# Own addresses for the seven feed-forward products

## The chip, the cores and the metric

The kernel runs on one core of one Trainium2 chip. The metric is the time of one execution on the device in microseconds (us); of several runs the median is given. TensorE multiplies matrices into the eight PSUM banks, VectorE (DVE) and ScalarE (ACT) work on tiles, GpSimd (POOL) does so too and issues some DMAs, SyncE (SP) issues most of them. SBUF holds 128 partitions; every address below is the byte address inside a partition.

## The reference

One layer of an encoder runs on two sequences (`x_prompt`, `x_sample`), each 1024 rows of 1024 numbers, with one set of float32 weights. Every sub-layer is shifted, scaled and gated by vectors that come from a conditioning input.

```python
h = rmsnorm(x, g_mix) * (1.0 + sc1) + sh1
z = h @ w_in                                   # latents for attention, and the Fourier input
mix = concatenate([mla_group(...), fourier_group(...)], axis=-1) @ w_out
x = x + ga1 * mix
h2 = rmsnorm(x, g_ffn) * (1.0 + sc2) + sh2
ffn = (silu(h2 @ w_gate) * (h2 @ w_up)) @ w_down   # 1024 -> 2816 -> 1024
return rmsnorm(x + ga2 * ffn, g_final)
```

The feed-forward part, the line with `w_gate`, `w_up` and `w_down`, is what the change touches.

## The kernel before

The kernel works in stages: weight preparation and projections, the Fourier part, attention with the output projection, and the feed-forward part. The feed-forward part runs from about 740 us to the end, first for sequence 0, then for sequence 1.

*Split operands.* Each float32 operand is held as two tiles, a rounded high part and the rest (`split`, lines 62 to 64: a cast on ACT, a subtraction on DVE). One product of two tiles is then three matmuls into the same bank (`mm3`, lines 79 to 81): high by high, high by low, low by high. In a matmul the first operand is the stationary 128x128 one that a weight load brings into the array ahead of it, the second the moving one of 512 columns.

*Seven products.* Each matrix product is done on 2x2 blocks in a form with seven block products and a few additions (numbers 0 to 6). In the first stage the moving operands are seven combinations of the normalised input, H[0] to H[6]. Each is held in two tiles (`H00` high, `H01` low, and so on) of 4 slices with 512 columns. They are made once per sequence by `prep_h` and stay. The stationary operands are combinations of `w_gate` and `w_up` for one block of 128 columns: seven tiles of 128x512, made into high and low parts by `hl` in buffers that turn through eight of each kind, `wh` and `wl`.

*First stage.* A sequence takes 22 passes. A pass does the products in the order 0, 5, 1, 6, 4, 3, 2 (`step`), 4 slices of 3 matmuls each, 12 matmuls a product, and uses three banks: x and y are added to again two products later, z likewise. Behind each product, `step` makes one tile of the next pass's weights with `hl`, and then a result is read out of a bank on ACT (lines 1704 and 1711) or DVE (line 1708 and `add`). Raw weights come by SP into four slots `X0` to `X3` (`slot`), two per pass, and POOL forms their sums. Results go to DRAM (`s_d`) by SP and POOL.

*Second stage.* `prod2` does one product of the down projection in 11 steps. Each step loads a tile a from `s_d` and a tile b from `w_down` or its sums, splits both with `hl` and does 4 x 3 matmuls: a gives the stationary slices, b is the moving tile. Seven products are 77 steps for sequence 0. Sequence 1 has 66, and its last product is done from tiles that were split ahead into H tiles that are no longer needed (`prep_last`, 132 matmuls). At the end of sequence 0, the weights for the first pass of sequence 1 are split by the line with `first_w`.

*Places.* Tiles lie in pools, one behind the other: H tiles and slots X on the left side of SBUF, `wh`, `wl`, two small tiles (`gf`, `tdb`) and 18 turning `val` tiles on the right. All H, X, wh and wl tiles are multiples of 512 bytes long, and all of them start at 64 modulo 512.

*Order.* The engines' programs are in the order that the framework's planner gives them. It places an instruction by when its operands are due. `issue_after` and `first` hold single instructions back.

Of the kernel before, what the change touches and what calls it, by code (L numbers as in the profile page):

```python
# [12 lines left out]
F32 = mybir.dt.float32  # L13
F32R = mybir.dt.float32r
# [7 lines left out]
P = 128  # L22
# [25 lines left out]
NTE = 258  # L48
NT = 514
NX = 2 * (NCOS + NNYQ)  # L50


@with_exitstack
def hybrid_encoder_kernel(ctx: ExitStack, tc: tile.TileContext, a: dict):
# [117 lines left out]
    zo = zp.tile([ZOW, NZC], F32, name="zo")  # L172
    zx = zp.tile([P, NX], F32, name="zx")
    zp.tile([P, 120], F32, name="gapz")
# [5 lines left out]
    with ExitStack() as st:  # L180
        p1b = st.enter_context(ExitStack())
        w2 = p1b.enter_context(tc.tile_pool(name="p1b", bufs=1, side="right", reuse_waits="tile"))
        w = st.enter_context(tc.tile_pool(name="p1", bufs=1, reuse_waits="tile"))
# [648 lines left out]
    S = {}  # L832
# [98 lines left out]
    with ExitStack() as st:  # L931
        early = st.enter_context(ExitStack())
        wa = early.enter_context(tc.tile_pool(name="p2a", bufs=1, reuse_waits="tile"))
        w = st.enter_context(tc.tile_pool(name="p2", bufs=1, side="right", reuse_waits="tile"))
# [293 lines left out]
    with ExitStack() as st:  # L1228
        w = st.enter_context(tc.tile_pool(name="p3", bufs=1, side="right", reuse_waits="tile"))
# [116 lines left out]
        for k in range(nit + 4):  # L1346
            if k >= nit:
                i = k - nit
# [7 lines left out]
            if k < nit:  # L1356
                s, b, h, u = items[k]
                scores(s, b, h, u)
                nxt = items[k + 8 - k % 8] if k + 8 - k % 8 < nit else None
                i = k % 8  # L1360
# [11 lines left out]
            if 0 <= k - 2 < nit and (k - 2) % 4 == 3:  # L1372
                s, b, h, u = items[k - 2]
# [17 lines left out]
    with ExitStack() as st:  # L1391
        w = st.enter_context(tc.tile_pool(name="p5", bufs=1, reuse_waits="tile"))
# [6 lines left out]
        def quad(tag, dt=F32):  # L1399
            return w.tile([P, 4, 512], dt, tag=tag, name=tag, bufs=1)  # L1400

        def slot(i, name="draw"):
            return w.tile([P, 2, 512], F32, tag=f"X{i % 4}", name=name, bufs=1)


        for tag in ("H20", "X0", "X1", "H21", "H30", "H31", "H00", "H41", "H01", "H50", "H51", "H10", "H11", "H40", "H60", "H61"):
            quad(tag) if tag[0] == "H" else [slot(2 * int(tag[1]) + i) for i in range(2)]

        def prep_h(H, s, n):

# [91 lines left out]
        H = {}  # L1502
# [13 lines left out]
        with tc.issue_after(S.pop(("tail", 4))):  # L1516
            w0 = sums_w([r[i // 2][:, i % 2, :] for i in range(4)], lambda i: wc[:, i, :], nc.vector)
# [27 lines left out]
        w5 = st.enter_context(tc.tile_pool(name="p5b", bufs=1, side="right", reuse_waits="tile"))  # L1545
# [5 lines left out]
        def val():  # L1551
            return w5.tile([P, 512], F32, tag="v", name="val", bufs=VALS)

        def hl(v):
            h = w5.tile([P, 512], F32R, tag="wh", name="wh", bufs=8)
            if "gf" not in S:
                S["gf"] = w5.tile([P, D], F32, name="gf")
                w5.tile([P, 2, 512], F32, tag="ga", name="tdb", bufs=1)
            l = w5.tile([P, 512], F32R, tag="wl", name="wl", bufs=8)
            split(h, l, v)  # L1560
            return h, l

        gf, first_w = None, None
        order = [fi + half * (NF // 2) for fi in range(NF // 2) for half in range(2)]
        pending = []
        turn = [0]
        for s in range(2):
            def combos(n, first=False, ahead=0):
                f = order[n]
# [68 lines left out]
                store_s(2, fi, v4, nc.gpsimd)  # L1638

            if s == 0:  # L1640
                wts = [hl(w0[i]) for i in range(4)]
                with behind():
                    for _ in range(2):
                        next(prep)
            else:
                wts = first_w
            A = {}
            late = None
            for n, f in enumerate(order):
                cur, nxt = wts, []  # L1650
                src = combos(n + 1, s == 0 and n == 0) if n + 1 < NF else None
                if late is not None:
                    put_s(*late)
                    late = None
                elif s == 0 and n > 0:
                    down_combos(n // 2)
                    if n % 4 == 1 and n < 20:
                        comb_h(1, n // 4 - 1) if n >= 5 else None

                def step(j, ps, k, first, src=src):  # L1660
                    prod(ps, k, cur[j], first)
                    if s == 0 and n == 0:
                        if j == 0:
                            cur.extend(hl(v) for v in w0[4:])
                            w0.clear()
                            S["n3"] = norm3(1, S.pop("jk3").bitcast(BF16))
                        if j < 3:
                            with behind():
                                for _ in range(2):
                                    next(prep, None)  # L1670
                            if j == 1:
                                with behind():
                                    S.pop("n3")()
                            return
                        if j == 3:
                            src = S["w1"] = sums_w(src, lambda i: val(), nc.vector)
                        src = S["w1"]
                        for i in ((), (), (), (0, 1), (2, 3), (4,), (5, 6))[j]:
                            nxt.append(hl(src[i]))
                        if j == 6:  # L1680
                            flip2(3, [S.pop(("xn", 1, 3, u)) for u in range(2)], bank, lambda g: val())
                    elif s == 1 and n == 0:
                        if j == 2:
                            with tc.issue_after(here["u2"]):
                                S["w1"] = sums_w(src, lambda i: val(), nc.vector)
                        with behind(), tc.issue_after(here["c"]) if j > 1 else ExitStack():
                            for i in ((), (), (0,), (1, 2), (3,), (4,), (5, 6))[j]:
                                nxt.append(hl(S["w1"][i]))
                        if j == 6:
                            S.pop("w1")  # L1690
                    elif src is not None:
                        nxt.append(hl(src[j]))
                    if s == 0 and n == 1 and j == 2:
                        S.pop("w1", None)

                def pend():
                    if pending:
                        with behind():
                            pending.pop(0)()

                x, y, z = bank(), bank(), bank()
                step(0, x, 0, True)
                p1 = val()
                here["c"] = nc.scalar.copy(p1, x).ins
                pend()
                step(1, y, 5, True)
                u2 = val()
                here["u2"] = nc.vector.tensor_tensor(out=u2, in0=y, in1=p1, op=ALU.add).ins  # L1708
                step(2, x, 1, False)
                sg = val()  # L1710
                nc.scalar.activation(sg, x, AF.Silu)
                pend()
                step(3, y, 6, False)
                u3 = val()
                add(u3, y, p1, nc.vector)
                step(4, z, 4, True)
                add(u3, z, u3, nc.vector)
                pend()
                step(5, y, 3, False)
                add(p1, y, p1, nc.vector)  # L1720
                nc.scalar.activation(p1, p1, AF.Silu)
                nc.vector.tensor_tensor(out=u3, in0=p1, in1=u3, op=ALU.mult)  # L1722
                step(6, z, 2, False)
                add(u2, z, u2, nc.vector)
                nc.vector.tensor_tensor(out=u2, in0=sg, in1=u2, op=ALU.mult)
                A[0, n % 2] = u2
                A[1, n % 2] = u3
                if n % 2 == 1:
                    late = (n // 2, A)
                    A = {}  # L1730
                wts = nxt
            put_s(*late)
            ga = w5.tile([P, D], F32, tag="ga", name="ga2", bufs=1)
            if gf is None:
                gf = S["gf"]
# [49 lines left out]
            def prod2(ps, k, first, last, hook=None, skip=0):  # L1785
                for f in range(NF // 2):
                    if f == NF // 2 - 1:
                        turn[0] -= skip
                    raw = slot(turn[0])
                    turn[0] += 1 + (skip if f == NF // 2 - 1 else 0)  # L1790
                    nc.sync.dma_start(raw[:, 0, :], s_d[s][k, f])
                    nc.sync.dma_start(raw[:, 1, :], bsrc(k, f))
                    ah, al = hl(raw[:, 0, :])
                    bh, bl = hl(raw[:, 1, :])
                    for t in range(4):
                        tt = slice(t * P, t * P + P)
                        mm3(ps[t], ah[:, tt], al[:, tt], bh, bl, first and f == 0, last and f == NF // 2 - 1, not first)
                    if hook is not None:
                        hook(f)
# [126 lines left out]
                    S["w0"] = combos(0, ahead=1)  # L1926

            prod2(Z, 2, False, True, hooks(steps, first_combos), 2)
            first_w = [hl(v) for v in S.pop("w0")]
            pending = rows_out(c11, u2, 0, 1, Z)  # L1930
            X = Y = Z = None
            H = Hn
# [109 lines left out]
```

## Time and profile before

| | |
|---|---|
| three runs | 2016.7, 2016.65, 2015.29 us; median 2016.65 us |
| profiled execution | span 2015.8 us from the first to the last instruction; the profile gives no other time for it |
| TensorE busy | 1973.1 us (98%), weight loads 1620.0 us (80%) |
| DVE, ACT, POOL busy | 1390.5 us (69%), 889.0 us (44%), 849.8 us (42%) |
| granted TensorE clock, mean | 0.995 |
| DMA | 376.59 MB, 187 GB/s on average |

A row of a group reads: line, engine, operation, written tile <- read tiles, shape, count, then the total and the mean time of one instruction, then the idle time of the engine ahead of them and what ended it. A row of a timeline reads: start and duration in us, engine, line, operation, tiles. Matmuls overlap on TensorE, so that the time of one is longer than the step from one start to the next; that step is called the pitch below. A row of windows reads: from:to, length, TensorE's busy time and its count of matmuls (any that reach into the window), granted clock, share and rate of the DMA engines.

### The profile page before, as it was taken

What the parts mean: (1) busy time and instruction counts of PE and PEld (TensorE: products, weight loads), DVE (VectorE), ACT (ScalarE), POOL (GpSimd) and SP (SyncE); (2) the same over time, 40 slices, a digit from 0 to 9 for tenths busy, and PEclk for the clock granted to TensorE, in tenths of its full rate; (3) what the DMA queues carried; (4) which work ended last, traced back from release to release, by engine and by line L of the source; (5) the groups of instructions that cost most, each with busy time, mean ns of one, the idle gap of its engine ahead of it and who ended that gap; (6) DMA issues with size and microseconds to landing.
All of it is one profiled execution on the core that took longest, in us unless ns stands there. A gap on an engine that the chain in (4) does not pass through costs nothing.

```text
span 2015.8 us, 27568 instructions
## 1 busy us (share of the span) xinstructions
PE 1973.1 (98%) x9526; PEld 1620.0 (80%) x9526; DVE 1390.5 (69%) x2064; ACT 889.0 (44%) x1720; POOL 849.8 (42%) x1012
## 2 busy tenths in 40 slices
PE   6899999999999999999999999999999999999998
PEld 3778778888888877888888888888888888888886
DVE  4557757766687678777777567788755655656784
ACT  2665535555565563333333356453333333335541
POOL 0654312111223237779779410344644554420152
PEclk8999999999999999999999999999999999999999
DMA  9785884445553575645646597665333333267762
GB/s 385 262 318 193 283 331 114 122 94 121 150 123 105 188 256 197 205 158 198 202 155 202 176 314 230 230 229 185 126 99 100 107 103 105 99 203 242 251 228 86
DMA packets 179449, 376.59 MB, mean 187 GB/s; under 512 B 17996, under 2 KB 57548, under 8 KB 175468
## 3 DMA queue, kind: packets, MB, share of 16 engines
q1 hardware_dynamic: 156908, 305.60, 45.3%
q0 software_dynamic: 21824, 68.17, 11.3%
q8 instruction: 75, 1.23, 0.2%
q10 hardware_dynamic: 576, 1.05, 0.1%
q14 instruction: 66, 0.54, 0.1%
HBM read 262.75 MB, written 120.39 MB: 190 GB/s over the span
## 4 chain that ended last, share of the span: by engine, by line
PE 59%; DVE 2%; issue 1%; POOL 1%; ACT 0%; POOLq 0%; DVEq 0%; ACTq 0%
PE bank L80 20%; PE bank L79 20%; PE bank L81 20%; DVE wl L64 1%; DVE val L152 0%; DVE val L1834 0%; DVE H L64 0%; DVE val L1806 0%; POOL rs_y L107 0%; DVE val L149 0%; POOL out_dram L1840 0%; DVE val L1722 0%; POOL rs_w L109 0%; POOL rs_w L110 0%; DVE val L1708 0%
## 5 line engine op out<-in xcount | busy, mean ns | idle before, releaser
L79 PE MATMUL bank<-H,wh 128*128 128x512 f32 x1232 | 480.8, 390 | 3.0 <-DVE val L152 1.3
L80 PE MATMUL bank<-H,wh 128*128 128x512 f32 x1232 | 480.0, 390 | 0.3 <-DVE H L64 0.3
L81 PE MATMUL bank<-H,wl 128*128 128x512 f32 x1232 | 479.8, 390 | 0.2 <-DVE wl L64 0.2
L79 PEld LDWEIGHTS bank<-H,wh 128*128 128x128 f32 x1232 | 231.4, 188 | 53.7 <-DVE val L152 2.6
L64 DVE TENSOR_TENSOR wl<-draw,wh 128x512 fp32r<-128x512 f32 x286 | 208.1, 764 | 90.9 <-ACT wh L63 90.2
L80 PEld LDWEIGHTS bank<-H,wh 128*128 128x128 f32 x1232 | 231.4, 188 | 48.4 <-DVE H L64 0.6
L81 PEld LDWEIGHTS bank<-H,wl 128*128 128x128 f32 x1232 | 231.4, 188 | 48.3 <-DVE wl L64 0.5
L152 DVE TENSOR_TENSOR val<-bank,val 128x512 f32<-128x512 f32 x200 | 136.6, 689 | 162.9 <-PE bank L81 162.3
L63 ACT CAST wh<-draw 128x512 fp32r<-128x512 f32 x286 | 165.1, 619 | 174.2 <-PE bank L80 129.4
L152 POOL TENSOR_TENSOR val<-val 128x512 f32<-128x512 f32 x58 | 81.0, 1398 | 344.2 <-DVE val L1806 164.5
L80 PE MATMUL bank<-wl,wh 128*128 128x512 f32 x572 | 223.3, 390 | 0.9 <-DVE wl L64 0.9
L81 PE MATMUL bank<-wh,wl 128*128 128x512 f32 x572 | 222.8, 390 | 0.0
L79 PE MATMUL bank<-wh 128*128 128x512 f32 x572 | 222.8, 389 | 0.0
L63 ACT CAST wh<-rgu 128x512 fp32r<-128x512 f32 x172 | 107.0, 622 | 257.4 <-PE bank L80 202.7
L63 ACT CAST wh<-val 128x512 fp32r<-128x512 f32 x133 | 82.2, 621 | 262.1 <-PE bank L80 244.9
L64 DVE TENSOR_TENSOR wl<-val,wh 128x512 fp32r<-128x512 f32 x133 | 125.7, 947 | 66.7 <-ACT wh L63 66.7
L64 DVE TENSOR_TENSOR wl<-rgu,wh 128x512 fp32r<-128x512 f32 x172 | 165.4, 961 | 1.4 <-ACT wh L63 1.4
L149 POOL TENSOR_TENSOR val<-rgu 128x512 f32<-128x512 f32 x80 | 107.8, 1347 | 79.4 <-DMA rgu<-in_wgu_dram 75.7
L80 PEld LDWEIGHTS bank<-wl,wh 128*128 128x128 f32 x572 | 107.5, 188 | 24.7 <-DVE wl L64 2.6
L79 PEld LDWEIGHTS bank<-wh 128*128 128x128 f32 x572 | 107.4, 188 | 22.5
L81 PEld LDWEIGHTS bank<-wh,wl 128*128 128x128 f32 x572 | 107.4, 188 | 21.9
L149 POOL TENSOR_TENSOR val<-val 128x512 f32<-128x512 f32 x89 | 119.3, 1358 | 1.3
(400 smaller groups left out, 3897.8 us busy)
## 6 DMA issues: line engine op xcount, KB each, us to landing
rgu<-in_wgu_dram SPq DMA_DIRECT2D x86, 512.0 KB, 4.0
draw<-s_d SPq DMA_DIRECT2D x143, 256.0 KB, 3.3
s_d<-val POOLq DMA_DIRECT2D x88, 256.0 KB, 3.2
draw<-t_d SPq DMA_DIRECT2D x88, 256.0 KB, 4.4
s_d<-val SPq DMA_DIRECT2D x66, 256.0 KB, 3.7
draw<-in_w_down_dram SPq DMA_DIRECT2D x55, 256.0 KB, 4.0
wada<-in_w_ada_dram SPq DMA_DIRECT2D x11, 1024.0 KB, 9.3
xt<-in_x_dram SPq DMA_DIRECT2D x16, 512.0 KB, 10.8
```

Of the source, the lines that this page charges most:

```text
L63: here["a"] = nc.scalar.copy(hi, src).ins
L64: here["v"] = (eng or nc.vector).tensor_tensor(out=lo, in0=src, in1=rd(hi), op=ALU.subtract).ins
L79: nc.tensor.matmul(out, lh, rh, start=first, stop=False, skip_group_check=cont)
L80: nc.tensor.matmul(out, lh, rl, start=False, stop=False, skip_group_check=cont)
L81: here["t"] = nc.tensor.matmul(out, ll, rh, start=False, stop=last, skip_group_check=cont).ins
L149: return eng.tensor_tensor(out=out, in0=x, in1=y, op=ALU.subtract).ins
L152: eng.tensor_tensor(out=out, in0=x, in1=y, op=ALU.add)
```

## The change

H tiles get untouched gaps in front of them, so that both tiles of H[k] start at `PLACE[k]` modulo 512. Each weight tile of the first stage gets a slot of its own, `wh0` to `wh6` and `wl0` to `wl6`, in the order of the products of a pass, at the place of its product; an eighth slot of each kind lies at 64. `hl` takes the number of the slot. In the second stage the tiles a and b take slots 0 and 1, then 2 and 3, 4 and 5, 6 and 7, and so on around (`spin`). `gf` and `tdb` stay between the two kinds, and are now placed when the pool is opened. No instruction, load or store is added or left out.

```diff
+PLACE = (64, 0, 32, 96, 128, 256, 160)
...
+        at = 64
+
+        def shift(pool, to):
+            nonlocal at
+            gap, at = (to - at) % 512, to
+            if gap:
+                pool.tile([P, gap // 4], F32, name=f"gap{len(gaps)}")
+                gaps.append(gap)
+
+        gaps = []
         for tag in ("H20", "X0", "X1", "H21", "H30", "H31", "H00", "H41", "H01", "H50", "H51", "H10", "H11", "H40", "H60", "H61"):
-            quad(tag) if tag[0] == "H" else [slot(2 * int(tag[1]) + i) for i in range(2)]
+            if tag[0] == "H":
+                shift(w, PLACE[int(tag[1])])
+                quad(tag)
+            else:
+                for i in range(2):
+                    slot(2 * int(tag[1]) + i)
...
-        def hl(v):
-            h = w5.tile([P, 512], F32R, tag="wh", name="wh", bufs=8)
-            if "gf" not in S:
+        spots = [PLACE[k] for k in (0, 5, 1, 6, 4, 3, 2)] + [64]
+        at = 64
+        for kind in "hl":
+            for i, spot in enumerate(spots):
+                shift(w5, spot)
+                w5.tile([P, 512], F32R, tag=f"w{kind}{i}", name=f"w{kind}", bufs=1)
+            shift(w5, 64)
+            if kind == "h":
                 S["gf"] = w5.tile([P, D], F32, name="gf")
                 w5.tile([P, 2, 512], F32, tag="ga", name="tdb", bufs=1)
-            l = w5.tile([P, 512], F32R, tag="wl", name="wl", bufs=8)
+
+        def hl(v, i):
+            h = w5.tile([P, 512], F32R, tag=f"wh{i}", name="wh", bufs=1)
+            l = w5.tile([P, 512], F32R, tag=f"wl{i}", name="wl", bufs=1)
             split(h, l, v)
             return h, l
...
-                        nxt.append(hl(src[j]))
+                        nxt.append(hl(src[j], j))
...
-                    ah, al = hl(raw[:, 0, :])
-                    bh, bl = hl(raw[:, 1, :])
+                    ah, al = hl(raw[:, 0, :], spin[0])
+                    bh, bl = hl(raw[:, 1, :], spin[0] + 1)
+                    spin[0] = (spin[0] + 2) % 8
...
-            first_w = [hl(v) for v in S.pop("w0")]
+            first_w = [hl(v, i) for i, v in enumerate(S.pop("w0"))]
```

More of the change, by code (lines that the diff above doesn't have):

```diff
@@ L1566, in hybrid_encoder_kernel @@
         turn = [0]
+        spin = [0]
         for s in range(2):
@@ L1640, in hybrid_encoder_kernel @@
             if s == 0:
-                wts = [hl(w0[i]) for i in range(4)]
+                wts = [hl(w0[i], i) for i in range(4)]
                 with behind():
@@ L1663, in step @@
                         if j == 0:
-                            cur.extend(hl(v) for v in w0[4:])
+                            cur.extend(hl(v, 4 + i) for i, v in enumerate(w0[4:]))
                             w0.clear()
@@ L1678, in step @@
                         for i in ((), (), (), (0, 1), (2, 3), (4,), (5, 6))[j]:
-                            nxt.append(hl(src[i]))
+                            nxt.append(hl(src[i], i))
                         if j == 6:
@@ L1687, in step @@
                             for i in ((), (), (0,), (1, 2), (3,), (4,), (5, 6))[j]:
-                                nxt.append(hl(S["w1"][i]))
+                                nxt.append(hl(S["w1"][i], i))
                         if j == 6:
```

## The prediction

> **What bounds the kernel now.** I read the page first: the shares of the span, the granted clock, the chain that ended last and the costliest groups.
>
> ```profile
> span 2015.8 us, 27568 instructions
> PE 1973.1 (98%) x9526; PEld 1620.0 (80%) x9526; DVE 1390.5 (69%) x2064; ACT 889.0 (44%) x1720; POOL 849.8 (42%) x1012
> PEclk8999999999999999999999999999999999999999
> PE bank L80 20%; PE bank L79 20%; PE bank L81 20%; DVE wl L64 1%; DVE val L152 0%; DVE val L1834 0%; DVE H L64 0%; DVE val L1806 0%; POOL rs_y L107 0%; DVE val L149 0%; POOL out_dram L1840 0%; DVE val L1722 0%; POOL rs_w L109 0%; POOL rs_w L110 0%; DVE val L1708 0%
> L79 PE MATMUL bank<-H,wh 128*128 128x512 f32 x1232 | 480.8, 390 | 3.0 <-DVE val L152 1.3
> L80 PE MATMUL bank<-wl,wh 128*128 128x512 f32 x572 | 223.3, 390 | 0.9 <-DVE wl L64 0.9
> L79 PE MATMUL bank<-H 128*128 128x512 f32 x44 | 17.1, 389 | 0.0
> ```
>
> TensorE is busy for 98% of the span at full clock, and 60% of the last chain is the lines 79 to 81 on `bank`, the feed-forward. Each of the three lines issues 1232 matmuls in the first stage (inputs H against weights wh, wl), 572 in the second, 44 at the end: 3 x 1848 = 5544. Their own 390 ns overlap, so what counts is the pitch from start to start. I took it from windows without a stall (a count holds some two matmuls that only reach into the window).
>
> ```profile
> 1450.00:1790.00 340.00, 340.00 (x1501) 1.00 0.32 106
> 1805.00:1950.00 145.00, 145.00 (x641) 1.00 0.76 252
> ```
>
> 340 us over 1499 is 226.8 ns in the first stage, 145 over 639 is 226.9 in the second: one pitch, whatever the DMA share (0.32 and 0.76). At it, 5544 matmuls are 1257 us. A nanosecond of pitch is 5.5 us, 0.27% of the span. Everything here hangs on whether the pitch knows addresses.
>
> Two views say that it is not a constant. The first is the timeline behind a stall.
>
> ```profile
> 926.78 0.40 PE L80 MATMUL bank<-H,wh 128*128 128x512 f32 x1
> ...
> 929.10 0.39 PE L81 MATMUL bank<-H,wl 128*128 128x512 f32 x1
> ```
>
> Ten pitches lie between these two rows: 2.32 us, 232.0 ns each, the same form as above. After a stall the pitch is thus 5 ns worse for some ten matmuls and then falls back to 226.8: a good rhythm that has to be found again, at about 10 x 5.2 = 52 ns for this one.
>
> The second is the Fourier input projection, where 128x256 slices of `wcs` run against `eoh` and `eol`. A row of `wcs` chunks is 536 floats, so each chunk of three matmuls starts 96 bytes further modulo 512. These are chunks one and six, twice, some 21 us apart.
>
> ```profile
> 94.40 0.28 PE L79 MATMUL bank<-wcs_h,eoh 128*128 128x256 f32 x1
> 94.78 0.28 PE L79 MATMUL bank<-wcs_h,eoh 128*128 128x256 f32 x1
> 96.19 0.28 PE L79 MATMUL bank<-wcs_h,eoh 128*128 128x256 f32 x1
> 96.53 0.28 PE L79 MATMUL bank<-wcs_h,eoh 128*128 128x256 f32 x1
> 115.44 0.28 PE L79 MATMUL bank<-wcs_h,eoh 128*128 128x256 f32 x1
> 115.81 0.28 PE L79 MATMUL bank<-wcs_h,eoh 128*128 128x256 f32 x1
> 117.22 0.28 PE L79 MATMUL bank<-wcs_h,eoh 128*128 128x256 f32 x1
> 117.56 0.28 PE L79 MATMUL bank<-wcs_h,eoh 128*128 128x256 f32 x1
> ```
>
> Three matmuls take 0.38 and 0.37 us at the first chunk, 0.34 and 0.34 at the sixth: 127 and 123 ns against 113 each. The difference comes back with the address, so a moving stream and the weight load beside it do depend on where they lie.
>
> **The change, part by part.** (a) *Inside a product of the first stage.* Before, H and weights all start at 64 modulo 512 (the diff's bookkeeping starts there). After, H[k] and the slots of product k share PLACE[k], so the distance between moving and stationary tile stays 0, and slices move by 2048 and 512 bytes, which keep it. If only the distance matters, 3696 matmuls stay at 226.8. No row shows a shared place other than 64, so the bounds: upwards the 5.2 ns above; downwards the 128x448 projection, one form in two states.
>
> ```profile
> 98.47 0.37 PE L79 MATMUL bank<-wz_h,eoh 128*128 128x448 f32 x1
> 100.75 0.37 PE L81 MATMUL bank<-wz_h,eol 128*128 128x448 f32 x1
> 106.00 0.36 PE L79 MATMUL bank<-wz_h,eoh 128*128 128x448 f32 x1
> 107.42 0.37 PE L80 MATMUL bank<-wz_l,eoh 128*128 128x448 f32 x1
> ```
>
> Eleven pitches in 2.28 us are 207.3 ns, seven in 1.42 us are 202.9: 4.4 ns lower. Six of seven products move, 3168 matmuls: -13.9 to +16.5 us. I take 0. The `wz` slices alternate between two places 256 bytes apart and hold 207.3, which speaks for a pitch that a shift alone does not alter.
>
> (b) *Switches of product.* 2 x 22 x 7 = 308 times the moving start jumps, and during the last matmul of one product the weights of the next load from another place. A rhythm that is lost costs up to the 52 ns above: 0 to 16.0 us, below nothing only with (a). I take one switch in six at 52 ns: +2.7 us, nearer to 0 because one odd load is less than a stall.
>
> (c) *The second stage.* The pair of slots for a and b goes round 64/256, 0/160, 128/96, 32/64, so the distance is no longer 0 in any pair: 1716 matmuls. By the same bounds -7.6 to +8.9 us. I take half of the upper one, +4.5 us: the one 128x512 rhythm that the trace shows away from 226.8 is the 232.0 ns one, and the address does matter by the `wcs` rows, but some pairs may find the better rhythm. The last product keeps both its operands in one H tile, 132 matmuls: 0, with 0.6 us on either side by the same bounds.
>
> (d) *Seven slots for eight turning buffers.* The cast of next weights j had the buffer of product j-1, and now waits for product j itself.
>
> ```profile
> 1000.05 0.39 PE L79 MATMUL bank<-H,wh 128*128 128x512 f32 x1
> 1000.08 0.62 ACT L63 CAST wh<-rgu 128x512 fp32r<-128x512 f32 x1 [1.59 <-PE bank L80]
> 1000.83 0.68 DVE L1708 TENSOR_TENSOR val<-bank,val 128x512 f32<-128x512 f32 x1
> 1001.43 1.18 DVE L64 TENSOR_TENSOR wl<-rgu,wh 128x512 fp32r<-128x512 f32 x1
> 1002.77 0.39 PE L79 MATMUL bank<-H,wh 128*128 128x512 f32 x1
> ```
>
> A product is 2.72 us. ACT already waits for TensorE at every product and casts 0.03 us into the next one; VectorE empties the bank before it subtracts. One product later the same beat carries the next tile, used five products on instead of six: 5 x 2.72 = 13.6 us against some 2.6 us (1000.08 to 1002.61). 0. Behind it on SP stand the loads of `rgu`, which wait for that subtraction, and then POOL's sums: all move by 2.72 us with their consumer, so no slack is used. If VectorE's order turned, it would cost (rival four).
>
> (e) *The seam between the sequences.* The first casts of sequence two ran ahead of the last tile of sequence one.
>
> ```profile
> 1375.98 0.62 ACT L63 CAST wh<-val 128x512 fp32r<-128x512 f32 x1
> 1376.11 0.69 DVE L64 TENSOR_TENSOR wl<-val,wh 128x512 fp32r<-128x512 f32 x1
> 1376.33 0.39 PE L81 MATMUL bank<-wh,wl 128*128 128x512 f32 x1
> 1376.56 0.39 PE L79 MATMUL bank<-H,wh 128*128 128x512 f32 x1
> 1376.58 0.62 ACT L63 CAST wh<-rgu 128x512 fp32r<-128x512 f32 x1
> 1376.71 0.69 DVE L64 TENSOR_TENSOR wl<-rgu,wh 128x512 fp32r<-128x512 f32 x1
> ```
>
> With 77 tiles the pair index ends at 76 x 2 modulo 8 = 0, so the last tile sits in slots 0 and 1, and the cast into slot 0 waits for its last read: start at 1376.58 instead of well before, end 1377.20, subtraction to about 1378.0. The third matmul needs it and would have started at 1376.56 + 2 x 0.227 = 1377.01: +1.0 us (0.6 to 1.2). Behind it on ACT the other casts follow at half a microsecond, faster than a product uses them.
>
> (f) *Gaps.* No instruction, no DMA. The tiles lie up to 2 KB further on the left, up to 4 KB lower on the right, over other old tiles; the stage's entry can shift by the idle time of L79 above, 3.0 us, at most: I take 0, -1 to +1.
>
> Sum: 0 + 2.7 + 4.5 + 0 + 1.0 + 0 = +8.2 us on a span of 2015.8, 2024.0. The median of the runs, 2016.65, stands 0.85 above that span (which is all that the profile gives of its execution's time): 2024.9, rounded down to 2024 because most of the sum rests on lost rhythm, whose terms can share a cause.
>
> **Rivals.** *No change in pitch.* Only (e) is left: 2016.65 + 1.0 = 2017.7. For it: one pitch in both stages under all loads. Against: the `wcs` rows. The Trainium skill, page "TensorE: Matmul & The Clock Gate", section "Step-by-step: what each phase is for", says that TensorE reads moving data and weights through two independent ports, so that the next weight load takes nothing from the running matmul; by that rule this rival is the outcome, and the `wcs` rows (127 against 113 ns by place) do not agree with it.
>
> *Faster.* One mechanism: a place other than 64 gives a pitch as much lower as the 128x448 states differ, in half of the moved products: 1584 x 4.4 ns = 7.0 us, less the 1.0 of (e): 2010.7; in all, and in the second stage too, 2016.65 - 13.9 - 7.6 + 1.0 = 1996. It decides from 1.3 ns a matmul on those 3168. Against: 226.8 is the lowest pitch that any 128x512 row here shows.
>
> *Much slower.* Every switch and every pair loses the rhythm, and shifted places too: 2016.65 + 16.5 + 16.0 + 8.9 + 1.0 = 2059; switches and pairs alone, 2042.6.
>
> *VectorE between bank and bank.* If it subtracted first, the bank would be empty at 0.03 + 0.62 + 1.18 + 0.68 = 2.51 us of a product's 2.72, and a slow subtraction would stop TensorE: 0.3 us in 44 passes, 13 us, 2030. Against: the order in the rows of (d).
>
> **How the numbers follow.** Forecast 0.45; no change in pitch 0.31; faster 0.18; much slower 0.04; VectorE 0.02. About 0.2%, 4 us, is what a measurement of this kernel can tell from no change: below 2012.6 lies most of "faster", 0.17; within, the second case and the edge of the first and third, 0.33; above, 0.50. The forecast's own range is 2020 to 2033 (2.7 and 4.5 replaced by their upper halves: 8.0 + 6.7 + 1.0 = 15.7). The range for 8 in 10 takes in the second case and the milder half of the third: 2008 to 2033.
>
> **What would show it.** A window inside the first stage at 226.8 for every product shows (a) right; a product with its own pitch, wrong. Pitches near 232 in the first matmuls after each switch show (b). Windows of the second stage: 145 us over some 632 matmuls show (c) in part, over 639 show it wrong. At the seam a stall of 1 us before the third matmul shows (e). The waits of ACT for L80 should keep their total, and L1708 should stand before L64. What would make the prediction wrong is a pitch that follows the place itself and not the distance.

## The result, and the profile after

The changed kernel takes 2033.3 us (median of 4 runs, 2030.95 to 2036.84) against 2016.68 for the kernel before beside it (2015.29 to 2016.8, 4 runs): a ratio of 1.0083, 95% interval 1.0071 to 1.0095. That is 16.6 us more, where 2024, some 8 us more, was forecast. The profiled execution took 2033.57 us with a span of 2031.5, 15.7 us above the span of before.

The page after has the same picture as before. Its lines are numbered one higher (`mm3` is now 80 to 82).

```profile
span 2031.5 us, 27501 instructions
PE 1990.9 (98%) x9526; PEld 1619.4 (80%) x9526; DVE 1399.6 (69%) x2064; ACT 889.8 (44%) x1720; POOL 845.1 (42%) x1012
L80 PE MATMUL bank<-H,wh 128*128 128x512 f32 x1232 | 481.6, 391 | 1.8 <-DVE val L1733 0.7
L81 PE MATMUL bank<-wl,wh 128*128 128x512 f32 x572 | 226.4, 396 | 0.4 <-DVE wl L65 0.2
```

TensorE carries 17.8 us more busy time with the same 9526 matmuls, more than the whole added span. No engine took over, and the waits did not grow in sum: idle time ahead of the six groups of matmuls of the two stages is 4.2 us, against 4.4 before (1.8 and 0.4 us ahead of the two shown). A matmul's own time went from 390 to 391 ns in the first stage and from 390 to 396 in the second. The windows give the pitch. The columns are from:to, length, TensorE's busy time with its count, granted clock, DMA share and rate.

```profile
1450.00:1790.00 340.00, 340.00 (x1488) 1.00 0.31 103
1815.00:1950.00 135.00, 135.00 (x581) 1.00 0.74 243
```

Less the two matmuls that only reach in, 340 us over 1486 is 228.8 ns in the first stage (226.8 before) and 135 over 579 is 233.2 in the second (226.9). The granted clock is 1.00 in both, so TensorE's clock was not lower: each matmul starts later after the one ahead of it.

The timeline shows where. These are the first matmuls of the seven products of one first-stage pass, and of the next pass (start and duration in us).

```profile
1538.43 0.39 PE L80 MATMUL bank<-H,wh 128*128 128x512 f32 x1
...
1541.17 0.39 PE L80 MATMUL bank<-H,wh 128*128 128x512 f32 x1
...
1543.90 0.39 PE L80 MATMUL bank<-H,wh 128*128 128x512 f32 x1
...
1546.63 0.39 PE L80 MATMUL bank<-H,wh 128*128 128x512 f32 x1
...
1549.40 0.39 PE L80 MATMUL bank<-H,wh 128*128 128x512 f32 x1
...
1552.16 0.39 PE L80 MATMUL bank<-H,wh 128*128 128x512 f32 x1
...
1554.90 0.39 PE L80 MATMUL bank<-H,wh 128*128 128x512 f32 x1
...
1557.64 0.39 PE L80 MATMUL bank<-H,wh 128*128 128x512 f32 x1
```

The pass takes 19.21 us, against 84 x 226.7 = 19.04. In six of the seven products the pitch starts out longer and comes back to 227 ns after three to nine matmuls; product 1 has it from its first. The excess is in the matmuls around the switches, in four cases in the last one ahead of a switch too (235 to 237 ns). Taken from the trace's starts as medians over 19 passes of sequence two, the switches cost 34, 12, 0, 51, 32, 32 and 12 ns (into products 0, 5, 1, 6, 4, 3, 2): 0.174 us a pass.

In the second stage the pitch never settles at 227. These are the first matmuls of five tiles in turn; the pairs lie at 0/160, 128/96, 32/64 and 64/256 (weights/moving).

```profile
1874.56 0.39 PE L80 MATMUL bank<-wh 128*128 128x512 f32 x1
...
1877.37 0.39 PE L80 MATMUL bank<-wh 128*128 128x512 f32 x1
...
1880.15 0.40 PE L80 MATMUL bank<-wh 128*128 128x512 f32 x1
...
1882.95 0.39 PE L80 MATMUL bank<-wh 128*128 128x512 f32 x1
...
1885.75 0.39 PE L80 MATMUL bank<-wh 128*128 128x512 f32 x1
```

Four tiles take 11.19 us: 48 matmuls at 233.1 ns. The seam between the sequences has the new stall.

```profile
1382.57 0.40 PE L82 MATMUL bank<-wh,wl 128*128 128x512 f32 x1
1382.82 0.62 ACT L64 CAST wh<-rgu 128x512 fp32r<-128x512 f32 x1 [0.28 <-PE bank L81]
...
1383.49 0.51 PE L80 MATMUL bank<-H,wh 128*128 128x512 f32 x1 [0.53 <-ACT wh L64]
...
1383.83 0.39 PE L81 MATMUL bank<-H,wh 128*128 128x512 f32 x1
1384.06 0.46 PE L80 MATMUL bank<-H,wh 128*128 128x512 f32 x1
...
1384.36 0.50 PE L82 MATMUL bank<-H,wl 128*128 128x512 f32 x1
```

The cast into a slot of the last tile is released by that tile's L81 and ends at 1383.44; TensorE waits for it. Over the four long steps that follow 1382.57, TensorE loses 0.99 us.

The difference of the two traces, by the starts of the 5544 feed-forward matmuls (us):

| stretch | before | after | difference |
|---|---|---|---|
| up to the first feed-forward matmul | 740.01 | 738.49 | -1.5 |
| sequence one, first stage | 425.96 | 427.85 | +1.9 |
| sequence one, second stage | 210.59 | 217.14 | +6.6 |
| sequence two, first stage | 420.05 | 423.92 | +3.9 |
| sequence two, second stage | 180.41 | 185.14 | +4.7 |
| last product, from the H tiles | 29.69 | 30.16 | +0.5 |
| behind the last matmul | 9.09 | 8.75 | -0.3 |

The pitch accounts for 7.3 + 11.0 + 0.5 = 18.8 us (mean of the steps under 260 ns, less that of before, times 3696, 1716 and 132). Longer steps, the stalls, are 1.2 us less in sum, the seam included, and the rest is the two ends. Since the first feed-forward matmul of the kernels below falls anywhere from 736.5 to 740.3 us, those 1.5 us are not put down to the change.

### The profile page after: what moved, and what is told of

The parts are those of the page before. It is cut to its first block, busy times and chain, and to the rows that moved or that the text cites. A ratio compares the mean times of both kernels' runs of the same rounds, so it can differ in the third digit from the quotient of the medians.

```text
span 2031.5 us, 27501 instructions
## 1 busy us (share of the span) xinstructions
PE 1990.9 (98%) x9526; PEld 1619.4 (80%) x9526; DVE 1399.6 (69%) x2064; ACT 889.8 (44%) x1720; POOL 845.1 (42%) x1012
## 4 chain that ended last, share of the span: by engine, by line
PE 60%; DVE 2%; POOL 1%; DMA 0%; issue 0%; ACT 0%; SPq 0%; POOLq 0%; DVEq 0%; ACTq 0%
PE bank L81 20%; PE bank L82 20%; PE bank L80 20%; DMA draw<-in_w_down_dram 0%; DVE wl L65 0%; DVE val L1832 0%; DVE val L1750 0%; DVE val L153 0%; DVE H L65 0%; POOL rs_y L108 0%; DVE val L150 0%; POOL out_dram L1866 0%; ACT wh L64 0%; POOL rs_w L110 0%; POOL rs_w L111 0%
## 5 line engine op out<-in xcount | busy, mean ns | idle before, releaser
L81 PE MATMUL bank<-H,wh 128*128 128x512 f32 x1232 | 481.9, 391 | 1.3 <-DVE H L65 1.3
L81 PEld LDWEIGHTS bank<-H,wh 128*128 128x128 f32 x1232 | 231.4, 188 | 52.3 <-DVE H L65 1.5
L81 PE MATMUL bank<-wl,wh 128*128 128x512 f32 x572 | 226.4, 396 | 0.4 <-DVE wl L65 0.2
L65 DVE TENSOR_TENSOR wl<-rgu,wh 128x512 fp32r<-128x512 f32 x172 | 159.1, 925 | 58.7 <-ACT wh L64 58.5
L64 ACT CAST wh<-val 128x512 fp32r<-128x512 f32 x133 | 82.5, 621 | 226.8 <-PE bank L81 217.4
L65 DVE TENSOR_TENSOR wl<-val,wh 128x512 fp32r<-128x512 f32 x133 | 130.3, 980 | 0.0
L81 PEld LDWEIGHTS bank<-wl,wh 128*128 128x128 f32 x572 | 107.3, 188 | 27.6 <-DVE wl L65 1.9
```

The source lines that it names most:

```text
L64: here["a"] = nc.scalar.copy(hi, src).ins
L65: here["v"] = (eng or nc.vector).tensor_tensor(out=lo, in0=src, in1=rd(hi), op=ALU.subtract).ins
L81: nc.tensor.matmul(out, lh, rl, start=False, stop=False, skip_group_check=cont)
```

## The experiments

Theory: the pitch depends on the distance between the start of a matmul's moving tile and the start of the weights that are loaded beside it, modulo some number of bytes. Tiles at distance 0 are called matched. When both move to another place (a jump), some matmuls have a longer pitch until it settles again: a transient. Rivals: the seven slots and the changed plan cost the time; places other than 64 do; turning through many places does. All edits are against the changed kernel.

**All slots, one place.** The slots and `spin` stay, the gaps go.

```diff
-PLACE = (64, 0, 32, 96, 128, 256, 160)
+PLACE = (64, 64, 64, 64, 64, 64, 64)
-        spots = [PLACE[k] for k in (0, 5, 1, 6, 4, 3, 2)] + [64]
+        spots = [64, 64, 64, 64, 64, 64, 64, 64]
```

> The changed kernel with every place put back to 64: only the seven fixed slots and the seam between the sequences remain of the change. Distance theory (the pitch follows the distance between the moving tile and the weights loaded beside it, modulo some power of two, and a jump of the place upsets it for some matmuls): pitch 226.7 ns in both stages, a stall of 0.7 to 1.0 us at the seam, 2016 to 2018 us. Slot rival (fixed slots turn the order of casts, subtractions and bank reads, and that costs the time): about 2033 us, and a pitch above 228 in the first stage.

Measured: 2019.48 us, ratio 1.0008 (0.9998 to 1.0018). The windows, as above:

```profile
1450.00:1790.00 340.00, 340.00 (x1502) 1.00 0.32 105
1815.00:1950.00 135.00, 135.00 (x597) 1.00 0.76 249
```

340/1500 and 135/595 are 226.7 and 226.9 ns: the pitch of before in both stages. The slots are not the cause of the pitch. The seam's stall is here too (1.63 us), so that belongs to the slots.

**One other place.** All products, slots and H tiles at 160 (`PLACE` and `spots` all 160).

> All H tiles and all sixteen weight slots at 160 modulo 512, a place that is no multiple of 64: no distance, no jump, another place. Distance theory: 226.7 ns in both stages, 2014 to 2018 us (the shifted tiles may save or cost up to 1.5 us at the stage's entry). Place rival (the place itself sets the pitch, 64 being a good one): 5 ns more for 5544 matmuls, 2040 us or above.

Measured: 2020.69 us, ratio 1.0013 (1.0002 to 1.0023). One pass of the first stage, first and last row:

```profile
1532.59 0.39 PE L80 MATMUL bank<-H,wh 128*128 128x512 f32 x1
...
1551.63 0.39 PE L80 MATMUL bank<-H,wh 128*128 128x512 f32 x1
```

19.04 us: 84 pitches of 226.7 ns at place 160. The second stage has 226.9 ns (mean of its steps under 260 ns). So place 160 by itself does nothing to the pitch.

**Many places, matched pairs.** The tiles a and b of a pair share a place, and the pairs still turn.

```diff
+PLACE = (64, 0, 32, 160, 160, 64, 0)
+        spots = [64, 64, 0, 0, 160, 160, 32, 32]
```

> Places 64, 64, 0, 0, 160, 160, 32, 32 for slots 0 to 7, and H tiles at the place of their product: in the second stage a and b of a step always share a place, but the place changes from step to step; in the first stage four of seven switches jump. Distance theory: switches cost about 12 (64 to 0), 51 (0 to 160), 0 to 51 (160 to 32) and 34 ns (32 to 64), as such jumps did in the changed kernel: some 127 ns in 44 passes, 5.6 us, and 127 ns in each four of the second stage's steps, a mean pitch of 229.3 there, 4.9 us; 2022 to 2029 us in all. Rival (what costs in the second stage is the turning through places, whatever the distance in a pair): 233 ns there as in the changed kernel, 2031 to 2035 us.

Measured: 2026.51 us, ratio 1.0036 (1.0024 to 1.0048). Five tiles of the second stage in turn (pairs at 0, 160, 32, 64):

```profile
1869.04 0.39 PE L80 MATMUL bank<-wh 128*128 128x512 f32 x1
...
1871.78 0.39 PE L80 MATMUL bank<-wh 128*128 128x512 f32 x1
...
1874.55 0.39 PE L80 MATMUL bank<-wh 128*128 128x512 f32 x1
...
1877.28 0.39 PE L80 MATMUL bank<-wh 128*128 128x512 f32 x1
...
1880.03 0.39 PE L80 MATMUL bank<-wh 128*128 128x512 f32 x1
```

10.99 us for 48, against 11.19 in the changed kernel and 10.88 at 226.7. Of the 6.5 ns that the second stage lost, this kernel loses only 2.2, in the transients at its four jumps in a round of tiles; the other 4.3 go with the distance within the pair. What the changed kernel's own jumps add can't be separated from that here: the settled pitches of its four distances, in the table below, leave nothing for them. In the first stage, neighbours with one place switch for 0 ns; its four jumps cost 12, 51, 10 and 34 ns, where the changed kernel had 12, 51 and 34 for the same jumps.

**Two places 256 apart.** Weights and moving tile match within a product; in the second stage a lies at 64 and b at 320.

```diff
+PLACE = (64, 64, 64, 320, 64, 320, 320)
+        spots = [64, 320, 64, 320, 64, 320, 64, 320]
```

> Places 64 and 320 by turns for the slots, H tiles at the place of their product: in the second stage a and b always stand 256 bytes apart, in the first stage six of seven switches jump by 256. Distance theory with a period of 256 bytes (the jump from 256 to 0 cost nothing in the changed kernel): 226.7 ns everywhere, 2014 to 2018 us. Distance theory with a period of 512 bytes: the second stage at 232 to 234 ns, 10 us more, 2025 to 2029 us.

Measured: 2018.77 us, ratio 1.0003 (0.9991 to 1.0016).

```profile
1450.00:1790.00 340.00, 340.00 (x1501) 1.00 0.32 105
1815.00:1950.00 135.00, 135.00 (x597) 1.00 0.78 250
```

The second stage runs at 226.9 ns with a distance of 256 in every pair, and six jumps of 256 a pass cost nothing. So 256 bytes count as no distance; the next runs show that none of the smaller distances tried does.

**Distances one by one.** Two kernels with all weights of the first stage at 64 and each H[k] at a distance of its own, products 0, 5, 1, 6, 4, 3, 2 in turn: 0, 256, 64, 128, 192, 32, 320 in the first; 96, 160, 224, 288, 352, 384, 448 in the second. Second-stage pairs all at 64. Each was run once.

> All weight slots at 64; the H tiles of products 0, 5, 1, 6, 4, 3, 2 lie 0, 256, 64, 128, 192, 32 and 320 bytes above that, so that the first stage measures one distance between moving tile and weights per product. Distance theory with a period of 256: products 0 and 5 settle at 226.7 ns; 192 near 233 as the pair 64/256 of the changed kernel did; 64 and 320 alike; 32 not settled, 231 to 235. First stage 4 to 6 ns above before on five of seven products: 11 to 17 us more, second stage at 226.7, 2028 to 2034 us. Place rival: nothing to say on distance, all products at 226.7 as in the run with all tiles at 160.

> As the run before it with other distances: 96, 160, 224, 288, 352, 384 and 448 bytes for products 0, 5, 1, 6, 4, 3, 2. Distance theory with a period of 256: 288 as 32, 352 as 96, 384 as 128, 448 as 192 in the run before; none below 226.7 ns; all seven products above it by 4 to 7 ns, 15 to 26 us more, 2032 to 2043 us. A distance that settles below 226.7 ns would be a gain to build on.

Measured: 2033.55 and 2044.2 us, beside 2020.12 of the kernel before. First matmuls of the products of one pass in the first of the two:

```profile
1539.85 0.39 PE L80 MATMUL bank<-H,wh 128*128 128x512 f32 x1
...
1542.59 0.39 PE L80 MATMUL bank<-H,wh 128*128 128x512 f32 x1
...
1545.31 0.40 PE L80 MATMUL bank<-H,wh 128*128 128x512 f32 x1
...
1548.08 0.40 PE L80 MATMUL bank<-H,wh 128*128 128x512 f32 x1
...
1550.87 0.39 PE L80 MATMUL bank<-H,wh 128*128 128x512 f32 x1
...
1553.67 0.39 PE L80 MATMUL bank<-H,wh 128*128 128x512 f32 x1
...
1556.46 0.40 PE L80 MATMUL bank<-H,wh 128*128 128x512 f32 x1
...
1559.22 0.39 PE L80 MATMUL bank<-H,wh 128*128 128x512 f32 x1
```

The lengths are 2.74 (distance 0, with a transient), 2.72 (256), 2.77 (64), 2.79 (128), 2.80 (192), 2.79 (32) and 2.76 (320). The second kernel's window shows that no distance in it is good: 340 us over 1455 is 233.7 ns.

```profile
1450.00:1790.00 340.00, 340.00 (x1457) 1.00 0.31 101
```

The settled pitch (mean of a product's sixth to eleventh step, 19 passes of each sequence), by moving start minus weight start modulo 256:

| distance | 0 | 32 | 64 | 96 | 128 | 160 | 192 | 224 |
|---|---|---|---|---|---|---|---|---|
| pitch, ns | 226.7 | 233.6 | 228.9 | 234.2 | 232.5 | 233.8 | 233.3 | 233.3 |

Single steps turn through a pattern about these means (225 to 241 ns), so tenths of a nanosecond say little. 288, 320, 352, 384 and 448 give within 1 ns what 32, 64, 96, 128 and 192 give. None lies below 226.7, so none of these distances makes the kernel faster.

**The same two places turned round.** Places 256 and 64 only; in the second stage the weights lie at 256 and the moving tile at 64.

```diff
+PLACE = (256, 256, 256, 64, 256, 64, 64)
+        spots = [256, 64, 256, 64, 256, 64, 256, 64]
```

> Only two places are left, 256 and 64, in turn, and every product of the first stage has H and weights at one of them; in the second stage the weights lie at 256 and the moving tile at 64 in every pair, the first pair of the changed kernel (weights 64, moving 256, 233.2 ns) turned round. Theory: the pitch follows the signed distance moving minus weights modulo 256; 64 - 256 is -192, which is +64 modulo 256, for which the first sweep showed 229 ns. So 229.0 in the second stage, +2.3 ns x 1716 = 4.0 us; six jumps of 192 per pass at 12 to 33 ns are 3.2 to 8.7 us; seam 1.0 to 1.6: about 2017.2 + 10.5 = 2027 us. Rival: only the size of the distance counts (192, as in the pair 64 and 256): 233.2 ns, +11.2 us in the second stage, about 2035 us.

Measured: 2026.88 us, ratio 1.0043 (1.0028 to 1.0058). Four tiles of the second stage, first and last row:

```profile
1866.56 0.39 PE L80 MATMUL bank<-wh 128*128 128x512 f32 x1
...
1877.55 0.39 PE L80 MATMUL bank<-wh 128*128 128x512 f32 x1
```

10.99 us for 48 is 229.0 ns, as a distance of +64 gives, and not the 233.2 of the same pair the other way: the sign counts. So it does in the jumps, which cost 12 ns by +192 and 42 by -192.

**The changed kernel, other pairs.** Places, slots and first stage untouched; the second stage pairs the same eight slots otherwise, at distances 0, 0, 192 and 160 modulo 256.

```diff
+        pairs = ((0, 7), (1, 2), (3, 5), (4, 6))
...
-                    ah, al = hl(raw[:, 0, :], spin[0])
-                    bh, bl = hl(raw[:, 1, :], spin[0] + 1)
+                    ah, al = hl(raw[:, 0, :], ia)
+                    bh, bl = hl(raw[:, 1, :], ib)
```

> All places as in the changed kernel, first stage untouched; only the second stage takes the same eight slots in other pairs: 0 with 7 (both at 64), 1 with 2 (256 and 0), 3 with 5 (160 and 96), 4 with 6 (128 and 32), distances 0, 256, 64 and 96 modulo 256 (moving minus weights: 0, 0, 192, 160). Theory that only the distance within a pair sets the pitch: 226.7, 226.7, 233 and 233 ns, mean 229.9 against 233.2 of the changed kernel, -3.3 x 1716 = -5.7 us, plus a transient of 12 to 50 ns at the jumps into the two matched pairs (+0.9 to 3.6 us): 2028.5 to 2031 us. Rival, that the turning through places itself costs what the second stage lost: no change, 2033.

Measured: 2032.79 us, ratio 1.0070 (1.0055 to 1.0086), above what was expected. Five tiles in turn, from the pair of slots 1 and 2:

```profile
1876.01 0.39 PE L80 MATMUL bank<-wh 128*128 128x512 f32 x1
...
1878.75 0.39 PE L80 MATMUL bank<-wh 128*128 128x512 f32 x1
...
1881.54 0.40 PE L80 MATMUL bank<-wh 128*128 128x512 f32 x1
...
1884.35 0.40 PE L80 MATMUL bank<-wh 128*128 128x512 f32 x1
...
1887.12 0.39 PE L80 MATMUL bank<-wh 128*128 128x512 f32 x1
```

2.74, 2.79, 2.81 and 2.77 us: the two matched pairs (first and last) are shorter, as far as a transient lets them. Taken tile by tile, the pair of slots 0 and 7 settles at 226.7 ns while that of 3 and 5 stays at 233.3, in one and the same turning through places, which the rival does not allow. The mean pitch of the stage is 231.5 ns against 233.2, 2.9 us less. But stalls in sequence one's second stage grew from 1.7 to 4.0 us, and the whole time does not differ from the changed kernel's 2033.3 us: the repair shows in the pitch alone. In sequence two, without such stalls, the stage took 183.36 us instead of 185.14.

**Only the two matched pairs.** `pairs = ((0, 7), (1, 2))`, all else as in the last one.

> All places as in the changed kernel, first stage untouched; the second stage uses only two pairs in turn, slots 0 with 7 (both at 64) and 1 with 2 (256 and 0), both at distance 0 modulo 256. Theory: the second stage falls back to 226.7 ns inside a tile, -11.2 us, but each change of pair is a jump of 64 or 192, 12 to 33 ns for 143 tiles (1.7 to 4.7 us): 2024 to 2027 us; what stays above 2017 is the switches of the first stage (7.7 us) and the seam. Rival: with two pairs instead of four the splits come late and TensorE stalls at each tile: above 2033.

Measured: 2063.73 us, ratio 1.0218 (1.0193 to 1.0243): the rival of late splits. The pitch outside stalls is 229.1 ns, so the distance did its part, but the list of TensorE's waits (total, times, longest in us) says what ate it:

```profile
PE bank L81 <- DVE wl L65: 21.2, 23, 2.0
```

With the steps behind them, stalls are 38 us in the two second stages. Two pairs are too few buffers; this run says little on places.

**The seam.** All places 64, and `spin = [2]`, so that the last tile of sequence one lies in slots 2 and 3.

> All places 64, and the round of pairs in the second stage starts at slots 2 and 3, so that the last tile of the first sequence lies in slots 2 and 3 and not in 0 and 1. Theory: the pitch is 226.7 throughout, and the seam's stall (1.63 us in the kernel with all places at 64) goes, because the first weight tile of sequence two has a free slot: about 2018 us, same as before. Rival: the stall stays because the split of the first tile waits for VectorE's or ScalarE's other work, and the time stays at the 2019.5 of the kernel with all places at 64.

Measured: 2028.29 us, ratio 1.0051 (1.0032 to 1.007), which is what neither the theory nor the rival gave. The seam's stall shrank from 1.63 to 0.79 us, but the second stage of sequence one now starts badly:

```profile
1183.75 0.35 SPq L1817 DMA_DIRECT2D draw<-in_w_down_dram  x1
1186.82 1.66 ACT L64 CAST wh<-draw 128x512 fp32r<-128x512 f32 x3 [11.09 <-DMA draw<-in_w_down_dram]
...
1187.49 0.50 PE L80 MATMUL bank<-wh 128*128 128x512 f32 x1 [4.08 <-ACT wh L64]
```

One load of the second stage is issued at 1183.75 and TensorE stands for 4.2 us; behind that, seven steps take 0.43 us each, in a window (1187 to 1193) with a granted clock of 0.72. The profile puts 2.8 us of SP's wait ahead of this issue down to the landing of an H tile's load; why that was late was not pursued. The first stage of sequence one takes 429.6 us, against 426.3 in the kernel with all places at 64, which is not explained either. The seam cannot be priced by this kernel alone.

## Where the prediction was right and where wrong

**Right in kind: the pitch knows addresses by distance.** The `wcs` rows showed that places matter; that it is the distance was an assumption of the prediction, and the runs bear it out: the kernels with matched tiles and no jump but of 256 bytes run at 226.7 to 226.9 ns, unmatched tiles at 228.9 or more. The sign that the prediction named for its being wrong, a pitch that follows the place itself, did not come. The Trainium skill, page "TensorE: Matmul & The Clock Gate", section "Step-by-step: what each phase is for", gives moving data and weights two independent read ports and says that loading the next weights takes no read bandwidth from the running matmul. The trace does not bear out that the load is free (233.2 against 226.9 ns for the second stage's same matmuls with other addresses), and the measurement decides. The rival built on it (2017.7) falls.

**(a) Inside a product, 0: right.** All seven places settle at 227 ns, and place 160 alone gives 226.7. With that the faster rival falls, which needed 1.3 ns a matmul.

**(b) Switches, 2.7 us: too small by 5.** The step that failed is "one switch in six at 52 ns". All but the one of 256 bytes (5 to 1) cost something: 0.174 us a pass, over 44 passes 7.7 us; the windows give (228.8 - 226.8) x 3696 = 7.4. As a ceiling for one switch the 52 ns held (51 was the dearest here), with some luck: it was read from rows rounded to 0.01 us, and the same ten steps take 2327 ns by the trace's starts, 60 ns too many. 7.7 lies within the bounds of 0 to 16.0. Why a jump was less than a stall was only asserted; nothing in the trace said that five in six would be free.

**(c) Second stage, 4.5 us: too small by 6.5, and its upper bound too low.** The step that failed is the bound, 5.2 ns taken from the transient behind a stall. Unrounded, those steps are 6.0 ns too long, which would have made the bound some 10 us, still below what came. Nothing made a transient's mean a ceiling for a rhythm that lasts: the pairs of the changed kernel run at 231.9 to 234.2 ns, 6.4 ns a matmul above before, 11.0 us. Halving the bound because "some pairs may find the better rhythm" failed as well: the distances are 192, 160, 224 and 32, and all of these stand at 233.3 ns or more in the table. What it needed, the price of a steady unmatched pair, no 128x512 row of before showed.

**(d) Slots, 0: nearly right.** The three kernels with slots and a single distance stand at ratios of 1.0003, 1.0008 and 1.0013, that is 0.6 to 2.6 us, seam included. Their traces have 3.5 to 4.8 us of stalls in sequence one's second stage and the step into the seam, against 1.0 before and 1.7 in the changed kernel, so the slots and the plan that goes with them are not quite free there. The waits of ACT for TensorE did not keep their total (577.0 us before, 648.7 after, over the three groups of casts into `wh`), but in the changed kernel TensorE's own waits did not grow in sum. VectorE still empties the bank first, 0.22 us behind the start of the cast (0.24 before, medians), so that rival falls too.

**(e) Seam, 1.0 us: right**, 0.99, with some luck in the size: the same stall is 1.63 us with all places at 64, outside the 0.6 to 1.2 given. It began at the first matmul, not at the third: the high part's cast was late as well.

**(f) Entry, 0: within what run and kernel vary by.** In the profiled execution -1.5 us at the start, -2.2 in stalls other than the seam's and -0.3 at the end hide part of the loss.

With 7.7 for (b) and 11.0 for (c), and the last product's 0.5, the prediction's own sum would be 2016.65 + 7.7 + 11.0 + 0.5 + 1.0 = 2036.9, and 2032.9 with what the start, the other stalls and the end gave back; measured were 2033.3. So the mechanism is that of the milder form of the rival "much slower" (every switch and every pair, 2042.6), whose price was too high for a switch by half and too low for a pair by 2 us.

## What to carry to other kernels

When matmuls with a weight load each run back to back, the runs speak for this: keep the moving tile's start and the stationary tile's start equal modulo 256 bytes, and keep the place from one product to the next; in this kernel's 128x512 form, breaking this cost 2.8% of the second stage's matmul time (233.2 against 226.8 ns) without any wait in the profile. Look for it as a lower count of matmuls in a window that is fully busy at full clock. And a mean over a transient was not an upper bound for a steady state here: price a state that lasts by a row that lasts, or widen the range.

## What the runs showed of the hardware

- The pitch of these matmuls has a period of 256 bytes in the distance of moving tile and weights, with a sign: +64 gives 229.0 ns, -64 (which is 192) gives 233.2.
- A jump of the shared place costs a transient that depends on the jump modulo 256: 0 ns at 256, 10 at -128, 12 at -64 (and +192), 32 at -32, 34 at +32, 42 at +64 (-192), 51 at +160, spread over up to ten matmuls.
- The last matmul ahead of a jump is already longer for jumps of 32 and 160 (median 235 to 237 ns) and of 128 (233), not for 64 and 192: it runs beside the weight load from the new place.
- What makes the pitch depend on the distance is not shown; the runs show the dependence only.
